# Two double-bank PSUM tiles taken in turn by a pair's first products, and a gate row that is turned on TensorE before it is written

## The chip, the cores and the metric

The kernel runs on one core of one Trainium2 chip. The metric is device time in microseconds (us) of one execution. Three runs of the kernel before gave 1339.73, 1339.51 and 1337.06 us, with a median of 1339.51. The profiled execution is another one, and took 1336.35 us.

## The reference, cut to what matters

One decoder block over 1024 tokens of width 1024. A vector `c` modulates the normed input, one wide projection feeds two mixers, and their gated sum goes through a last matrix:

```python
mod = jax.nn.silu(c) @ ada_w[l] + ada_b[l]
shift, scale, gate = jnp.split(mod, 3, axis=-1)
h = rms_norm(x, norm_w[l]) * (1.0 + scale[:, None]) + shift[:, None]
proj = h @ w_in[l]
...
merged = jax.nn.sigmoid(ga) * y_a + jax.nn.sigmoid(gb) * y_b
x = x + gate[:, None] * (merged @ w_out[l])
return rms_norm(x, final_norm_w)
```

Mixer A is a gated delta rule (a recurrence over chunks, 8 heads), mixer B a windowed attention. The change touches two places: how the columns of `proj` that hold the gates z and g are multiplied, and how `gate` gets from a column layout in SBUF to a row in DRAM.

## The kernel before, in words

Every large product is done in three passes of fp32r matmuls (high part by high, high by low, low by high), 512 columns each. The order of all instructions is worked out when the kernel is built: each part of the work is a generator ("stream") with a priority, and a planner (`Sched`, with a table of assumed durations) steps whichever stream of the highest priority it holds to be ready. What a stream issues in a step gets its place in the queue of its engine at once. On the chip each engine then keeps that order, and waits with semaphores where data or a buffer is not ready. The program records each instruction through one helper, so the profile puts all of them on line 106; they are told apart by their tiles.

Buffers are slots: `big` (34 tiles of 128x1024), `mid` (6 of 128x512), `sq` (6 of 128x128), `wr` and `wh` for raw and split weights. PSUM has two double-bank tiles `pj` (128x1024, 4 KiB in a partition) and four single-bank tiles `sb` (128x512).

**The pairs.** 14 pairs of weight tiles (z and most of g) are multiplied by a scheme of seven products in place of eight (`PRODUCTS`, line 32): each product is 4 k-tiles of 3 matmuls, 12 matmuls of 128x512. `pair` (line 661) issues them in order. Products 1 and 2 (into `ps["B11"]` and `ps["T2"]`) go to the two halves of one `pj` tile, products 3 and 4 (`T1`, `B21`) to the two halves of the other, and products 5 to 7 to `sb` tiles. A stream of higher priority, `pair_out` (line 695), follows and turns the products into four output blocks: as soon as a product is issued, its evacuation is issued. That is a copy on ScalarE (ACT) for the first product and an addition on VectorE (DVE) for each of the others, `mid<-mid,pj` in the profile. A `pj` tile is given back with `pj.put()` when the second of its two products has been read. Before the first pair, the operand T1 is prepared in `t1_part` (line 805); after the last pair, `h_blocks` (line 739) restores the blocks that the pairs had overwritten, and the first unit after the pairs waits for them.

**The modulation.** `ada_stream` (line 475) computes `mod` with one VectorE dot product per 128 rows of `ada_w`. After the normed input is ready, it does the last eight (the gate), halves them (line 492) and writes them with one DMA (line 493) from `mod[:, 16:24]`, 128 partitions with 8 elements each, to the row `row_d` in DRAM: the address pattern puts elements of one partition 512 B apart, so each of the 1024 elements of 4 B is a run of its own. The row is read once, near the end (`rows_stream`).

**What stands near it in the queues.** Right behind that DMA, SyncE's queue (SP) issues two loads `big<-grow` (`d_stream`, line 1165): 512 KB each, the decay logits of a head broadcast to 128 partitions. VectorE scans them (`tensor_tensor_scan`), and behind the scans in its queue come the key scales and the convolution of a key tile (`conv`, line 838: three `scalar_tensor_tensor` that read a `pj` tile, then `pj.put()`). The stream `stats_stream` (line 1099) does with a 128x64 tile what the change does with the gate: transpose on TensorE, ACT copy, DMA in rows (`grow<-sq`).

Of the kernel before, what the change touches and what calls it, by code (L numbers as in the profile page):

```python
# [9 lines left out]
AF = mybir.ActivationFunctionType  # L10
OP = mybir.AluOpType
# [4 lines left out]
P = 128  # L16
# [12 lines left out]
HALVES = (slice(0, 512), slice(512, 1024))  # L29
# [235 lines left out]
def hybrid_block_kernel(ctx: ExitStack, tc: tile.TileContext, x, c, norm_w, ada_w, ada_b, w_tiles, w_vb0, w_vb1,  # L265
# [3 lines left out]
    pe, act, dve, pool, sp = S.pe, S.act, S.dve, S.pool, S.sp  # L269
# [16 lines left out]
    sq = Slots(S, smp, "sq", 6, [P, P])  # L286
    pj = Slots(S, pjp, "pj", 2, [P, T])
    sb = Slots(S, sbp, "sb", 4, [P, 512])

    def const(shape, name, dtype=F32):  # L290
        return cp.tile(shape, dtype, name=name)
# [3 lines left out]
    ident, upper, later, ones = cst[:, 0:128], cst[:, 128:256], cst[:, 256:384], cst[:, 384:512]  # L295
# [10 lines left out]
    mod = const([P, 24], "mod")  # L306
# [28 lines left out]
    row_d = dp.tile([1, T], F32, name="rowd")  # L335
# [133 lines left out]
    def ada_dot(j, aw):  # L469
        mdt = yield from big.get()  # L470
        dve.scalar_tensor_tensor(mdt, aw, 1.0, scb[0], op0=OP.mult, op1=OP.mult, accum_out=mod[:, j:j + 1])
        dve.tensor_tensor(mod[:, j:j + 1], mod[:, j:j + 1], adab[:, j:j + 1], op=OP.add)
        big.put()

    def ada_stream():
        for kk in range(8):
            yield ev_mod
            for j in (8 + kk, kk):
                yield ev_aw[j]
                yield from ada_dot(j, aw[j])  # L480
                big.put()
            dve.scalar_tensor_tensor(A_d[:, kk:kk + 1], mod[:, 8 + kk:9 + kk], 1.0, nw_t[:, kk:kk + 1],
                                     op0=OP.add, op1=OP.mult)
            S.set(ada_ev[kk])
        yield ev_h[7][1]
        for j in range(16, 24):
            a_ = yield from big.get()
            sp.dma_start(a_, ada_w[j * P:(j + 1) * P, :])
            yield
            yield from ada_dot(j, a_)  # L490
            big.put()
        dve.tensor_scalar(mod[:, 16:24], mod[:, 16:24], 0.5, None, op0=OP.mult)
        sp.dma_start(row_d.rearrange("o (j p) -> p (o j)", p=P), mod[:, 16:24])
        big.put()

    todo_h = []
    for k_ in range(8 + LAG):
# [163 lines left out]
    def pair(u, blocks, ready, sink, free=None):  # L661

        nk = u.n // 2 // P
        ps = {}
        done = {b: Event() for _, b in PRODUCTS}
        S.add(pair_out(ps, done, sink), 8, "pairout")
        for n, (a, b) in enumerate(PRODUCTS):
            if n in (0, 2):  # L670
                two = yield from pj.get()
            if n > 3:
                pt = yield from sb.get()
            else:
                pt = two[:, HALVES[n % 2]]
            ps[b] = pt
            yield u.ev[a]
            w, v = u.part[a]
            for kt in range(nk):
                yield ready[b][kt]  # L680
                whi, wlo = w[:, kt * P:(kt + 1) * P], v[:, kt * P:(kt + 1) * P]
                hi, lo = blocks[b][kt]
                pe.matmul(pt, whi, hi, start=kt == 0, stop=False)
                pe.matmul(pt, whi, lo, start=False, stop=False)
                pe.matmul(pt, wlo, hi, start=False, stop=kt == nk - 1)
                if free:
                    free(b, kt)
                yield S.now()
            if a in ("S1", "A12", "A22"):
                wh.put(2)  # L690
            elif a == "S4":
                wh.put()
            S.set(done[b])

    def pair_out(ps, done, sink):
        def add(o, x, y):
            dve.tensor_tensor(o, x, y, op=OP.add)

        yield done["B11"]
        p, u, v = yield from mid.many(3)  # L700
        act.activation(p, ps["B11"], AF.Copy)
        yield done["T2"]
        add(u, p, ps["T2"])
        pj.put()
        yield done["T1"]
        add(v, u, ps["T1"])
        yield done["B21"]
        add(p, p, ps["B21"])
        pj.put()
        yield  # L710
        yield from sink(0, 0, p)
        yield done["T3"]
        add(p, v, ps["T3"])
        add(u, u, ps["T3"])
        sb.put()
        yield
        yield from sink(1, 1, p)
        mid.put()
        yield done["B22"]
        add(v, v, ps["B22"])  # L720
        sb.put()
        yield
        yield from sink(0, 1, v)
        mid.put()
        yield done["T4"]
        add(u, u, ps["T4"])
        sb.put()
        yield
        yield from sink(1, 0, u)
        mid.put()  # L730
# [267 lines left out]
    def projections():  # L998
# [41 lines left out]
        for n, (kind, idx, u) in enumerate(prog):  # L1040
# [3 lines left out]
            if kind == "two":  # L1044
                if n == LAST2:
                    yield from pair(u, HB, ev_hb, idx, h_free)
                    big.debt -= 1
                    S.set(ev_early)
                else:
                    yield from pair(u, HB, ev_hb, idx)  # L1050
                continue
# [944 lines left out]
    S.add(load_start(), 0, "load")  # L1996
    S.add(ln_start(), 0, "ln")
    S.add(ada_stream(), 1, "ada")
    S.add(h_stream(), 1, "ha")
    S.add(h_stream(), 1.1, "hb")  # L2000
# [94 lines left out]
```

## Time and profile before

| what | value |
|---|---|
| median of three runs | 1339.51 us |
| profiled execution | 1336.35 us, its span 1334.6 us |
| TensorE (PE) busy | 1252.5 us, 94% of the span |
| VectorE busy | 749.5 us, 56% |
| ScalarE busy | 532.1 us, 40% |
| GpSimd (POOL) busy | 382.6 us, 29% |
| 128x512 matmuls into pj | x3168, mean 404 ns of one |

A mean of 404 ns does not mean that a matmul begins every 404 ns: matmuls are pipelined, and in a stream a new one begins before the last has ended. In the timeline a row is a run of instructions of one kind on one engine: start, length, operation, shapes, count, and in brackets the idle time of the engine just before it and what ended that idle time. Engine names with a q are queues.

### The profile page before, as it was taken

The numbers are of one execution on the slowest core, as the hardware profiler recorded it, in microseconds if no ns is written. First come the engines' busy times: TensorE is split into PE (matmuls) and PEld (weight loads), VectorE is DVE, ScalarE is ACT, GpSimd is POOL, SyncE is SP. The second block draws the span as 40 slices with busy tenths as digits, with TensorE's granted clock in tenths as the row PEclk, the third lists the DMA queues.
The fourth block names the chain that finished last, engine by engine and source line by source line (L and its number), as shares of the span: only waits on it lengthen the run. The fifth ranks groups of instructions, "written<-read, shape, count | busy, mean of one in ns | idle before, by whom it ended". The sixth has DMA issues, their size and how long they took to land. (4 is left out here: it accounts for less than half of the span.)

```text
span 1334.6 us, 19368 instructions
## 1 busy us (share of the span) xinstructions
PE 1252.5 (94%) x7218; PEld 1028.3 (77%) x7218; DVE 749.5 (56%) x1412; ACT 532.1 (40%) x1140; POOL 382.6 (29%) x227
## 2 busy tenths in 40 slices
PE   5798899989999899999989999999999999999997
PEld 3597788857887677777768888888988767888886
DVE  6655688975556464644546787244442336756533
ACT  5545453333443343544436532355363452212211
POOL 4621854652122121311234511212124102222400
PEclk9899899989999999999989999999999999999999
DMA  9354547644444745542435634656856758653422
GB/s 362 131 177 125 177 132 218 215 141 145 150 130 159 218 135 162 187 155 71 135 127 159 196 103 150 214 166 215 244 178 200 243 182 227 198 185 123 142 95 95
DMA packets 141328, 225.79 MB, mean 169 GB/s; under 512 B 34193, under 2 KB 83761, under 8 KB 141234
## 3 DMA queue, kind: packets, MB, share of 16 engines
q1 hardware_dynamic: 141090, 224.29, 52.7%
q8 instruction: 57, 0.93, 0.3%
q14 instruction: 37, 0.30, 0.1%
q10 hardware_dynamic: 144, 0.26, 0.1%
HBM read 149.88 MB, written 74.63 MB: 168 GB/s over the span
## 5 line engine op out<-in xcount | busy, mean ns | idle before, releaser
L106 PE MATMUL pj<-big,wh 128*128 128x512 f32 x3168 | 806.8, 404 | 48.1 <-DVE mid L106 12.5
L106 PEld LDWEIGHTS pj<-big,wh 128*128 128x128 f32 x3168 | 587.6, 192 | 182.2 <-DVE mid L106 18.0
L106 POOL TENSOR_TENSOR wh<-wr,wh 128x1024 fp32r<-128x1024 f32 (+4 forms) x64 | 145.4, 2273 | 446.9 <-ACT wh L106 389.3
L106 ACT ACTIVATE wh<-wr 128x1024 fp32r<-128x1024 f32 (+4 forms) x110 | 104.2, 948 | 157.7 <-PE pj L106 112.5
L106 PE MATMUL sb<-big,wh 128*128 128x512 f32 x504 | 130.0, 402 | 0.2 <-DVE mid L106 0.2
L106 ACT ACTIVATE big<-big 128x1024 f32<-128x1024 f32 (+1 forms) x61 | 64.6, 1059 | 158.8 <-DVE big L106 126.9
L106 PE MATMUL pj<-wh,big 128*128 128x256 f32 (+2 forms) x702 | 107.2, 309 | 3.5 <-DVE big L106 1.8
L106 PEld LDWEIGHTS sb<-big,wh 128*128 128x128 f32 x504 | 91.3, 189 | 19.3 <-DVE mid L106 1.2
L106 PEld LDWEIGHTS pj<-wh,big 128*128 128x128 f32 x702 | 96.4, 193 | 10.8 <-issue 3.1
L106 DVE SCALAR_TENSOR_TENSOR big<-pj,cw,big 128x1023 f32<-128x1023 f32 (+2 forms) x66 | 84.5, 1280 | 29.9 <-ACT big L106 28.2
L106 POOL TENSOR_TENSOR big<-wr 128x512 f32<-128x512 f32 x14 | 20.6, 1471 | 243.0 <-DMA wr<-in_w_tiles_dram 166.0
L106 DVE TENSOR_TENSOR big<-big,big 128x1024 f32<-128x1024 f32 (+3 forms) x40 | 62.5, 1568 | 24.3 <-ACT big L106 13.0
L106 PEld LDWEIGHTS sb<-sq,big 128*128 128x128 f32 x464 | 65.0, 190 | 12.1 <-issue 3.2
L106 PE MATMUL sb<-sq,big 128*128 128x128 f32 x464 | 69.2, 278 | 2.5 <-DVE sq L106 2.0
L106 ACT ACTIVATE mid<-sb 128x384 f32<-128x384 f32 (+5 forms) x75 | 34.4, 461 | 81.3 <-PE sb L106 66.1
L106 DVE TENSOR_TENSOR mid<-mid,pj 128x512 f32<-128x512 f32 x42 | 28.8, 687 | 61.7 <-PE pj L106 57.3
L106 POOL TENSOR_TENSOR big<-mid,big 128x512 fp32r<-128x512 f32 x32 | 50.5, 1584 | 37.5 <-ACT big L106 22.3
L106 DVE TENSOR_TENSOR wh<-wr,wh 128x1024 fp32r<-128x1024 f32 (+1 forms) x46 | 51.9, 1131 | 7.4 <-ACT wh L106 7.2
L106 DVE TENSOR_TENSOR mid<-mid,sb 128x512 f32<-128x512 f32 x56 | 37.0, 682 | 33.3 <-DMA zd<-mid 14.3
L106 ACT ACTIVATE mid<-mid 128x512 f32<-128x512 f32 (+1 forms) x59 | 35.9, 609 | 47.7 <-DVE mid L106 47.3
L106 ACT ACTIVATE mid<-mid,sta 128x128 f32<-128x128 f32 (+1 forms) x96 | 42.1, 440 | 27.0 <-DVE sta L106 26.9
L106 DVE SCALAR_TENSOR_TENSOR sq<-sb,gsm,big 128x128 f32<-128x128 f32 x56 | 19.4, 348 | 53.3 <-PE sb L106 49.4
(138 smaller groups left out, 1451.2 us busy)
## 6 DMA issues: line engine op xcount, KB each, us to landing
wr<-in_w_tiles_dram SPq DMA_DIRECT2D x64, 512.0 KB, 4.1
rkd<-big SPq DMA_DIRECT2D x32, 512.0 KB, 4.5
big<-rkd SPq DMA_DIRECT2D x64, 256.0 KB, 3.5
big<-in_ada_w_dram SPq DMA_DIRECT2D x24, 512.0 KB, 9.0
big<-in_x_dram SPq DMA_DIRECT2D x16, 512.0 KB, 4.6
big<-gd SPq DMA_DIRECT2D x16, 512.0 KB, 4.9
zd<-mid SPq DMA_DIRECT2D x28, 256.0 KB, 3.3
big<-zd SPq DMA_DIRECT2D x14, 512.0 KB, 7.5
```

The costliest lines, as they stand in the source:

```text
L106: r = f(*a, **k)
```

## The change

The first four products of a pair take the two `pj` tiles in turn: product 1 the lower half of the first tile, product 2 the lower half of the second, products 3 and 4 the upper halves. Both tiles are taken before the second product, and the first tile is given back after the third product's addition, where it was after the second's.

The gate is no longer halved on VectorE. Its 128x8 tile is transposed on TensorE into an `sb` tile, copied with a factor of 0.5 by ScalarE into an `sq` tile of 8 rows, and written from there, 8 rows of 512 B. The `big` tile that held the broadcast `c` is given back before these steps.

```diff
-        dve.tensor_scalar(mod[:, 16:24], mod[:, 16:24], 0.5, None, op0=OP.mult)
-        sp.dma_start(row_d.rearrange("o (j p) -> p (o j)", p=P), mod[:, 16:24])
         big.put()
+        yield
+        pb = yield from sb.get()
+        pe.transpose(pb[0:8, 0:P], mod[:, 16:24], ident)
+        yield
+        t = yield from sq.get()
+        act.activation(t[0:8, :], pb[0:8, 0:P], AF.Copy, scale=0.5)
+        sb.put()
+        yield
+        sp.dma_start(row_d.rearrange("o (j p) -> (o j) p", p=P), t[0:8, :])
+        sq.put()
...
-        ps = {}
+        ps, two = {}, []
...
         for n, (a, b) in enumerate(PRODUCTS):
-            if n in (0, 2):
-                two = yield from pj.get()
+            if n < 2:
+                two.append((yield from pj.get()))
             if n > 3:
                 pt = yield from sb.get()
             else:
-                pt = two[:, HALVES[n % 2]]
+                pt = two[n % 2][:, HALVES[n // 2]]
...
         add(u, p, ps["T2"])
-        pj.put()
         yield done["T1"]
         add(v, u, ps["T1"])
+        pj.put()
         yield done["B21"]
         add(p, p, ps["B21"])
         pj.put()
```

## Prediction

> **What bounds the kernel now.** I read the page first, then the waits of TensorE, then the timeline around the two places that the change touches.
>
> ```profile
> span 1334.6 us, 19368 instructions
> PE 1252.5 (94%) x7218; PEld 1028.3 (77%) x7218; DVE 749.5 (56%) x1412; ACT 532.1 (40%) x1140; POOL 382.6 (29%) x227
> L106 PE MATMUL pj<-big,wh 128*128 128x512 f32 x3168 | 806.8, 404 | 48.1 <-DVE mid L106 12.5
> ```
> ```profile
> PE pj L106 <- DVE big L106: 13.5, 6, 8.6
> PE pj L106 <- DVE mid L106: 12.5, 14, 2.4
> PE pj L106 <- ACT mid L106: 8.6, 11, 1.4
> ...
> PE pj L106 <- ACT big L106: 5.9, 3, 2.9
> ...
> PE sb L106 <- DVE sq L106: 4.7, 2, 2.7
> ```
>
> TensorE is the bound: no other engine is busy over 56%, and TensorE has only some 82 us in which it does nothing. So an idle microsecond of TensorE that goes away is worth nearly a microsecond of the end, as long as nothing else comes late in its place. The second list (total us, times, longest) tells where that idle time is. Two rows stand out by their counts: 14 waits for `DVE mid` and 11 for `ACT mid`, where the kernel has 14 pairs. And one wait is far longer than the rest: 8.6 us for `DVE big`. The change aims at exactly these.
>
> **The pairs.** One pair in the timeline:
>
> ```profile
> 400.55 2.32 PE L106 MATMUL pj<-big,wh 128*128 128x512 f32 x9
> 402.91 0.60 ACT L106 ACTIVATE mid<-pj 128x512 f32<-128x512 f32 x1 [1.01 <-PE pj L106]
> 403.56 5.05 PE L106 MATMUL pj<-big,wh 128*128 128x512 f32 x21 [0.69 <-ACT mid L106]
> 406.68 0.69 DVE L106 TENSOR_TENSOR mid<-mid,pj 128x512 f32<-128x512 f32 x1 [0.24 <-PE pj L106]
> 410.57 0.69 DVE L106 TENSOR_TENSOR mid<-mid,pj 128x512 f32<-128x512 f32 x1 [3.20 <-PE pj L106]
> 411.31 1.65 PE L106 MATMUL pj<-big,wh 128*128 128x512 f32 x6 [0.78 <-DVE mid L106]
> ```
>
> Product 1 ends; ACT copies it from 402.91 to 403.51, and only at 403.56 does product 2 begin. It goes to the other half of the same PSUM tile, so the program holds the write back until the read of the tile is over. Then 21 matmuls run without a break: 12 of product 2 and 9 of product 3. Product 2 is read by DVE at 406.68, in the midst of this run, and nothing waits: product 3 writes the other tile. Product 4 goes to the tile from which product 3 is being read (410.57), and waits again. So a write waits for a read of the same tile, whichever half, and not for one of the other tile. With the tiles taken in turn, product 2 no longer shares a tile with product 1, nor product 4 with product 3. The new neighbours are products 1 and 3, and 2 and 4, and between their turns lies a whole product.
>
> What one wait costs is more than its bracket:
>
> ```profile
> 280.71 3.01 PE L106 MATMUL pj<-big,wh 128*128 128x512 f32 x12 [0.75 <-ACT mid L106]
> 286.25 0.80 PE L106 MATMUL pj<-big,wh 128*128 128x512 f32 x1 [2.53 <-ACT big L106]
> ...
> 295.65 4.61 PE L106 MATMUL pj<-big,wh 128*128 128x512 f32 x12 [2.37 <-DVE mid L106]
> 300.10 8.36 PE L106 MATMUL sb<-big,wh 128*128 128x512 f32 x36
> 308.30 2.88 PE L106 MATMUL pj<-big,wh 128*128 128x512 f32 x12
> ...
> 677.58 0.73 PE L106 MATMUL pj<-big,wh 128*128 128x512 f32 x2 [2.94 <-ACT big L106]
> ```
>
> 36 matmuls without a break take 8.36 us, so one begins every 0.227 us ((8.36 - 0.40) / 35), while one lasts 0.404. The bracket is counted from the end of the last one, and leaves out 0.404 - 0.227 = 0.18 us that a stream would have overlapped. And 12 matmuls right after a wait take 3.01 us, others 2.88: 0.13 more. A wait thus costs its bracket and 0.31. All 25: 12.5 + 8.6 + 25 x 0.31 = 28.9 us.
>
> Two of them I take as not gained, 1.1 us each (0.75 or 0.78 and 0.31). In the first pair (280.71 to 295.65) product 3 waits 2.53 us for its operand T1, which ACT is still splitting (`ACT big`); a product 2 that begins earlier only lengthens that wait. After the last pair the next unit waits for restored blocks (677.58, 2.94 us), and a pair that ends earlier will wait the longer. So 26.7 us go.
>
> What is late next: product 3 now needs the copy of product 1, issued one product earlier, and product 4 needs the addition of product 2. A product is 12 x 0.227 = 2.7 us; the read takes 0.7, and the copy above began 0.04 us after the last matmul's end (402.87). So the reader may be some 1.7 us late (2.7 - 0.18 - 0.04 - 0.7, less the step between engines) before TensorE waits. The row at 295.65 shows that it can be: product 4 of the first pair waited 2.37 us, because DVE was in a long chain. And each recurrence step between the pairs loses the slack that a pair's waits gave it. I give back 3 us for all of this, near the 4.7 us in 2 waits that `DVE sq` costs now; the ends are 0 and 10 (about a third of what was won). **Pairs: 23.7 us.**
>
> [...]
>
> **The gate's row.**
>
> ```profile
> 113.28 0.16 DVE L106 TENSOR_TENSOR mod<-mod,adab 128x1 f32<-128x1 f32 x1
> 113.48 0.17 DVE L106 TENSOR_SCALAR mod<-mod 128x8 f32<-128x8 f32 x1
> 113.68 0.38 SPq L106 DMA_DIRECT2D rowd<-mod  x1
> 114.16 1.78 SPq L106 DMA_DIRECT2D big<-grow  x2
> ...
> 120.03 17.84 SPq L106 DMA_DIRECT2D rkd<-big  x2
> ...
> 122.83 6.64 PE L106 MATMUL pj<-big,wh 128*128 128x512 f32 x28
> 128.28 5.16 DVE L106 TENSOR_TENSOR_SCAN big<-big,cst 128x128 f32<-128x128 f32 x16 [14.63 <-DMA big<-grow]
> ...
> 134.05 3.91 DVE L106 SCALAR_TENSOR_TENSOR big<-pj,cw,big 128x1023 f32<-128x1023 f32 x3
> ```
> ```profile
> 138.10 9.14 PE L106 MATMUL pj<-big,wh 128*128 128x512 f32 x30 [8.63 <-DVE big L106]
> ```
> ```profile
> 114.00:123.00 9.00, 9.00 (x50) 7.62 (x49) 0.00 (x0) 8.69 (x29) 0.00 (x0) 1.00 0.18 12
> 123.00:129.50 6.50, 6.47 (x29) 4.99 (x27) 1.23 (x4) 3.92 (x11) 0.00 (x0) 1.00 0.86 215
> ...
> 138.00:142.00 4.00, 3.90 (x9) 3.14 (x10) 3.86 (x6) 3.04 (x11) 3.65 (x3) 0.50 0.72 183
> ...
> 280.00:680.00 400.00, 364.84 (x2173) 289.45 (x2173) 218.40 (x410) 160.96 (x361) 92.36 (x59) 0.98 0.49 153
> ```
> ```profile
> big<-grow SPq DMA_DIRECT2D x8, 512.0 KB, 6.5
> ...
> grow<-sq SPq DMA_DIRECT2D x1, 32.0 KB, 1.8
> ...
> rowd<-mod SPq DMA_DIRECT2D x1, 4.0 KB, 9.3
> ```
>
> The chain: the row's DMA is issued at 113.68 and lands 9.3 us later, at 123.0. The two loads behind it are issued at 114.16, but until 123 the DMA engines move 12 GB/s at 18% busy; from then on 215. The loads move only when the row is through, though the row is 4 KB. DVE stands idle for 14.63 us, scans from 128.28, reaches the convolution at 134.05 and frees the `pj` tile at 137.96; TensorE, out of work at 129.47, goes on at 138.10. And it goes on slowly: in the four microseconds after (column before the last two: granted clock 0.50) nine matmuls take what they would do in 9 x 0.227 = 2.0 us. The wait costs 8.63 + 0.31 + 2.0 = 10.9 us.
>
> After the change the row is 8 runs of 512 B. The nearest row is `grow<-sq`, the same kind of write from the same kind of tile, 64 rows, 32 KB: 1.8 us. The loads would land in the 6.5 us that is the median of all eight. If they are issued at 114.16 again, the scan begins near 120.7. From scan to the end of the convolution it is 137.96 - 128.28 = 9.7 us, so the tile is free near 130.4, where TensorE needs it at 129.5: 0.9 us of wait are left. With nothing else on the DMA engines the load can be faster, down to no wait; I take 0.5. An idle time this short does not slow what follows: the 2.53 us above lie in a stretch whose granted clock is 0.98.
>
> What is added:
>
> ```profile
> 101.26 0.30 PE L106 MATMUL sb<-cst,gsm 128*64 128x128 f32 x1 [0.61 <-DVE gsm L106]
> 101.80 0.25 ACT L106 ACTIVATE sq<-sb 64x128 f32<-64x128 f32 x1
> ```
>
> The model is the decay row in `stats_stream`: 0.30 us on TensorE with 0.61 us of wait, 0.25 us on ACT. The transpose stands in TensorE's order and everything of TensorE stands behind it, so if its place comes before DVE has finished `mod` (113.44) TensorE waits. Bounds: 0.1 us (pipelined, no wait) to 0.9. The four `sb` tiles are then in use by the key transposes, whose evacuations the planner must see first, so its place is a little later than 113.44; I take 0.4 with the ACT copy, which other ACT work covers. On SP the row's DMA now waits for ACT; behind it stand the writes `rkd<-big`, the second of which waits long anyway (17.84 us for the two). If the loads `grow` stay behind it, they are late by about the time of transpose, copy and their queues, some 3 us, and the price is 3 us of TensorE's wait. DVE loses 0.17 us, worth nothing. The row is read near the end of the span, so its landing does not matter. **Gate: 10.9 - 0.5 - 0.4 = 10.0 us.**
>
> **Sum.** 23.7 + 10.0 = 33.7 us. From the profiled execution, 1336.35 - 33.7 = 1302.7. That execution is 3.2 us below the median of the runs, so by the median 1339.5 - 33.7 = 1305.8: 1306.
>
> **Rivals.**
>
> The gate's half fails: the loads are slow for themselves, or the transpose costs as a new wait what the row's DMA cost. For it: the median landing of `big<-grow`, 6.5, is already not short. Against it: 12 GB/s until the moment the row lands. Time: 1339.5 - 23.7 = 1316. Chance 0.08.
>
> The pairs' half does nothing, because the wait hangs on something other than the tile. [...] Against it: product 3 runs through a read of the other tile. Time: 1339.5 - 10.0 = 1329.5. Chance 0.05.
>
> Slower, through the recurrence:
>
> ```profile
> L106 PE MATMUL sb<-sq,TT x112: 270/274/377, 343.6 to 1017.6; 128*128 128x128 f32 x112
> ```
>
> All orders are planned anew behind the change, and recurrence steps lie between the products. 112 such matmuls are 56 steps of two instructions each after the first of every head; each step has three links over DVE or ACT, 168 links. If TensorE, without the pairs' pauses, comes to every link over 0.2 us too early, 168 x 0.2 = 33.6 us, and the gain is gone; at 0.25 us the kernel takes 1339.5 + 8 = 1348. Against it: only 4.7 us in 2 such waits now. Chance 0.04. Half of that lateness, 0.1 us a link, gives 1306 + 17 = 1323, chance 0.03.
>
> [...] The clock of 0.98 from 280 to 680, with 25 pauses that the change removes, speaks against it: chance 0.01.
>
> **How the numbers follow.** My forecast has 0.77. Its own range is 1299 (nothing given back, no wait left: 28.9 - 2.2 + 10.9 = 37.6, and 3 us for runs as low as the profiled one) to 1313 (10 us given back). The range must reach the first rival, and ends at 1319. A measurement of this kernel can tell about 0.2% (2.7 us) from no change. Every case but two is faster by more; the slower one and the clock have 0.05, and no change has 0.02, the recurrence at its point of balance. So faster 0.93.
>
> **What would show it.** In the profile after: no `ACT mid` waits of `PE pj` or only one or two, and `DVE mid` under 4 us; `rowd<-sq` in the list of DMAs, landing in 2 to 3 us; the scan from about 120 us; no idle time of TensorE above 1 us between 100 and 200 us, and a granted clock near 1.0 there. Wrong would be: waits of the same count with other partners (products 3 and 4), the scan still at 128, more `DVE sq` waits than two, or a gap before a transpose `sb<-cst,mod`.

## The result, and the profile after

The kernel after takes 1304.46 us (median of 4 runs, 1303.67 to 1305.68). Beside it the kernel before has 1338.28 us (4 runs, 1335.88 to 1339.73). The ratio is 0.975, with a 95% interval from 0.9731 to 0.9768. The forecast was 1306, in a range of 1299 to 1319. The profiled execution after took 1305.68 us, 30.7 us less than the one before.

The page of the kernel after, its span, its engines and the group of the 128x512 matmuls:

```profile
span 1304.0 us, 19379 instructions
PE 1241.0 (95%) x7219; PEld 1027.7 (79%) x7219; DVE 756.8 (58%) x1411; ACT 532.0 (41%) x1141; POOL 380.4 (29%) x227
L106 PE MATMUL pj<-big,wh 128*128 128x512 f32 x3168 | 794.7, 401 | 27.1 <-ACT big L106 13.8
```

TensorE's idle time, span less busy, went from 82 to 63 us. Its busy time fell too, by 11.5 us, though it does one instruction more. A busy microsecond is not a fixed amount of work: in the kernel after a 128x512 matmul lasted 652 ns at a granted clock of 0.50 (649.94 to 653) and 389 ns at 1.00 (284 to 288), and the end of the last matmul ahead of a wait, of which a stream overlaps some 0.18 us (one of 0.404 us begins every 0.227), counts as busy. The waits of TensorE, kernel after (total us, times, longest):

```profile
PE pj L106 <- ACT big L106: 14.3, 4, 7.9
...
PE sb L106 <- DVE sq L106: 7.2, 2, 3.9
...
PE pj L106 <- DVE big L106: 4.2, 5, 2.1
...
PE pj L106 <- ACT mid L106: 0.7, 1, 0.7
```

Of the 14 waits for `DVE mid` before a `pj` product none is left, of the 11 for `ACT mid` one, and the 8.6 us for `DVE big` are gone. Two things have grown. `ACT big` has a wait of 7.9 us that was not there, and `DVE sq` has 7.2 where it had 4.7.

Around the modulation, the timeline of the kernel after:

```profile
108.01 0.80 SPq L106 DMA_DIRECT2D big<-grow  x2
113.73 5.16 DVE L106 TENSOR_TENSOR_SCAN big<-big,cst 128x128 f32<-128x128 f32 x16 [1.30 <-DMA big<-grow]
...
116.06 0.27 PE L106 MATMUL sb<-cst,mod 128*8 128x128 f32 x1
...
121.11 0.29 SPq L106 DMA_DIRECT2D rowd<-sq  x1
...
123.07 3.92 DVE L106 SCALAR_TENSOR_TENSOR big<-pj,cw,big 128x1023 f32<-128x1023 f32 x3 [1.76 <-ACT big L106]
```

The loads are now issued at 108.01, six microseconds earlier than before. SP's queue had stood at the row, which waited for `mod`; the row's place is now behind them. The scan begins at 113.73 (before: 128.28) and the convolution at 123.07 (134.05). The transpose waits for nothing. The windows of the kernel after (PE, PEld, DVE, ACT, POOL busy, granted clock, DMA share, GB/s):

```profile
129.50:138.00 8.50, 8.50 (x50) 7.40 (x49) 6.18 (x5) 6.87 (x14) 8.50 (x5) 1.00 0.25 80
138.00:142.00 4.00, 4.00 (x30) 3.60 (x29) 3.96 (x10) 1.00 (x6) 3.42 (x2) 1.00 0.55 152
280.00:680.00 400.00, 385.36 (x2303) 315.30 (x2302) 219.65 (x423) 171.62 (x383) 91.58 (x57) 0.98 0.49 155
```

From 129.5 to 138, where TensorE had stood, it is busy throughout, and from 138 to 142 it does 30 matmuls at a granted clock of 1.00 (most of them of 128x128) instead of nine at 0.50.

The first pair has a wait of a new kind. Timeline of the kernel after:

```profile
267.94 1.22 DVE L106 TENSOR_TENSOR big<-big,ik 128x1024 f32<-128x1024 f32 x1
...
269.19 0.32 SPq L106 DMA_DIRECT2D vrd<-big  x1
269.56 2.56 SPq L106 DMA_DIRECT2D mid<-t1d  x4
...
275.58 1.29 ACT L106 ACTIVATE big<-mid 128x512 fp32r<-128x512 f32 x2 [0.89 <-DMA mid<-t1d]
...
277.72 1.00 ACT L106 ACTIVATE big<-pj 128x1024 f32<-128x1024 f32 x1
...
278.78 10.09 PE L106 MATMUL pj<-big,wh 128*128 128x512 f32 x36 [7.88 <-ACT big L106]
288.70 3.56 PE L106 MATMUL sb<-big,wh 128*128 128x512 f32 x15
```

Read it from the bottom. Product 2 now needs the second `pj` tile, which still holds the result of the unit before. ACT copies that result out at 277.72. But in ACT's queue the copy stands behind the splits of T1, and these wait for the loads `mid<-t1d`. On SP those loads were issued only at 269.56, behind a store `vrd<-big` that waited for DVE. So TensorE stands for 7.88 us. Before, the same pair had four waits (0.75, 2.53, 0.63 and 2.37 us). Now it has one, and in this trace the pair as a whole is still 2.3 us shorter. That is not firm: in a second profile of the same kernel, from the run again below, the loads are issued at 271.69, the wait is 9.85 us, and the pair is 0.1 us longer than before.

**Where the time went**, by the starts and ends of the same instructions in both traces. Product 5 of the first pair starts at 300.10 before and at 288.70 after, 11.4 us earlier. Of these, 1.0 us had been won by the transpose of the decay row (101.26 and 100.25), 8.1 came from there to the first pair, 2.3 in it. From product 5 of the first pair to the end of product 7 of the last it takes 369.3 and 350.2 us, 19.1 less. From there to the end of the span 665.2 and 665.1. Sum: 30.6 us of span. Each of these is a difference of two single executions.

### The profile page after: what moved, and what is told of

The parts are those of the page before. It is cut to its first block, busy times and chain, and to the rows that moved or that the text cites. A ratio compares the mean times of both kernels' runs of the same rounds, so it can differ in the third digit from the quotient of the medians.

```text
span 1304.0 us, 19379 instructions
## 1 busy us (share of the span) xinstructions
PE 1241.0 (95%) x7219; PEld 1027.7 (79%) x7219; DVE 756.8 (58%) x1411; ACT 532.0 (41%) x1141; POOL 380.4 (29%) x227
## 4 chain that ended last, share of the span: by engine, by line
PE 43%; DVE 4%; DMA 2%; issue 1%; ACT 0%; SPq 0%; POOL 0%; POOLq 0%; DVEq 0%; ACTq 0%
PE pj L106 35%; PE sb L106 8%; DVE big L106 3%; DVE mid L106 1%; DMA mid<-fgd 1%; DMA big<-rkd 1%; DMA ogd<-mid 0%; ACT big L106 0%; DVE qpart L106 0%; SPq L106 0%; DVE fga L106 0%; POOL big L106 0%; ACT mid L106 0%; POOLq L2099 0%; ACT wh L106 0%
## 5 line engine op out<-in xcount | busy, mean ns | idle before, releaser
L106 PE MATMUL pj<-big,wh 128*128 128x512 f32 x3168 | 794.7, 401 | 27.1 <-ACT big L106 13.8
L106 PE MATMUL pj<-big,big 128*128 128x512 f32 x210 | 49.1, 389 | 0.0
```

What stands on the lines that cost most here:

```text
L106: r = f(*a, **k)
```

## The experiments

In each, "after" is the kernel after and "before" the kernel before; ratios are to the kernel before, timed beside it.

### The pairs' half alone

The kernel before, with the change's edits in `pair` and `pair_out` and none in `ada_stream`:

```diff
-            if n in (0, 2):
-                two = yield from pj.get()
+            if n < 2:
+                two.append((yield from pj.get()))
...
-                pt = two[:, HALVES[n % 2]]
+                pt = two[n % 2][:, HALVES[n // 2]]
```

> The kernel before with the pairs' half of the change alone; the gate's row stays as it was. Theory (a write to a PSUM tile waits for a read of the same tile, whichever half): the 14 waits for DVE mid and 11 for ACT mid of PE pj go, the 8.6 us wait for DVE big at 138 us stays, and about 21 us are won: 1338.3 - 21 = 1317. Rival (the gain of the change comes from the new order that the planner makes, not from the tiles): much less than 15 us is won here, because the order is much as before up to the pairs.

1321.18 us, ratio 0.9857 (0.9835 to 0.9878): 18.4 us less. The waits for `ACT mid` and `DVE mid` before a `pj` product are gone, and the one behind the row stays (timeline of this kernel):

```profile
138.58 3.64 PE L106 MATMUL pj<-big,wh 128*128 128x512 f32 x9 [9.52 <-DVE big L106]
```

So this half does what it says by itself. It gains less than the 23.7 of the forecast, in part for reasons taken up below, and in part because this kernel has a wait of its own, 3.77 us for `ACT wh` at 310.23.

### The gate's half alone

The kernel before, with the change's edits in `ada_stream` alone:

```diff
-        sp.dma_start(row_d.rearrange("o (j p) -> p (o j)", p=P), mod[:, 16:24])
...
+        pe.transpose(pb[0:8, 0:P], mod[:, 16:24], ident)
...
+        act.activation(t[0:8, :], pb[0:8, 0:P], AF.Copy, scale=0.5)
...
+        sp.dma_start(row_d.rearrange("o (j p) -> (o j) p", p=P), t[0:8, :])
```

> The kernel before with the gate's half alone. Theory (the two loads of decay logits stood behind the row's 1024 runs of 4 B): the wait of 8.6 us at 138 us goes and the clock stays up there, about 10 us are won: 1338.3 - 10 = 1328. The 25 waits in the pairs stay. Rival (the halves hang together: time won before the pairs is lost again at the first pair, where the operand T1 is late): 1334 or more, with a longer wait at the first pair.

1331.98 us, ratio 0.9934 (0.9913 to 0.9954): 7.6 us less. No wait is left at 138. But the first pair has a longer one (timeline of this kernel):

```profile
281.76 6.12 PE L106 MATMUL pj<-big,wh 128*128 128x512 f32 x15 [6.41 <-ACT mid L106]
```

TensorE comes to the first pair earlier and there waits 6.41 us where it had waited 0.75, for the copy of product 1, which stands in ACT's queue behind the splits of T1. A part of this half's gain is given back there. The halves add up to 26.0 us, and together they bring 33.8; the product of their ratios, 0.979, lies just above the interval of the whole. The 6.41 us here and the 3.77 us of the pairs' half are waits that the kernel after does not have.

### Another neighbour in the tile

The kernel after, where products 2 and 3 share a tile instead of 1 and 3, 2 and 4:

```diff
-                pt = two[n % 2][:, HALVES[n // 2]]
+                pt = two[n in (1, 2)][:, HALVES[n // 2]]
```

> The changed kernel, but product 3 goes to the upper half of the second tile and product 4 to that of the first: product 2 and product 3 are neighbours in one tile, all four still lie in four banks, and products 1 and 2 and 3 and 4 are still in different tiles. Theory (guard by tile): product 3 waits for the addition that reads product 2, about 13 or 14 waits for DVE mid of 0.8 us, 0.18 to 0.31 us more each: 13 to 15 us slower than the changed kernel, 1304.5 + 14 = 1318. Rival (the guard goes by bank, and the waits of before came from something else about products 2 and 4): no such waits, 1304.5.

1322.38 us, ratio 0.9866 (0.9845 to 0.9887). By the ratios (0.975 for the kernel after) some 15.5 us are lost. The waits of TensorE in this kernel:

```profile
PE pj L106 <- DVE mid L106: 11.3, 13, 1.3
```

All that differs in the code is which half of which tile a product takes. Thirteen waits come with it, 11.3 us in all, one in nearly every pair, at product 3, whose neighbour is being read. The program holds back a write to a tile while any part of it is read. Products 2 and 3 lie in different halves of the tile. Whether the chip would do without these waits was not tried; the program's guard is per tile, and that is what costs here.

### The copy of the unit before ahead of T1

The kernel after, where the splits of T1 are issued only when the copy that frees the second tile has been:

```diff
+    ev_evac = Event()
-        yield ev_last[i]
+        yield [ev_last[i], ev_evac]
...
+        if store is KB and i == 1:
+            S.set(ev_evac)
```

> The changed kernel, with the ScalarE splits of T1 held back, in the order of issue, until the copy is issued that frees the second PSUM tile before the first pair. Theory (the new wait of 7.9 us at the first pair is the second tile, asked for one product earlier than before, and its copy stands in ScalarE's queue behind splits that wait for late loads): product 2 of the first pair begins within 1.5 us of product 1's end, product 3 then waits some microseconds for T1, and the first pair ends 3 to 6 us earlier: 1304.5 - 4.5 = 1300. Rival (what is late is T1 itself, and the wait only moves from product 2 to product 3): 1304.5 within 1.

1313.44 us, ratio 0.9796 (0.9776 to 0.9815): about 6 us slower than the kernel after, where I had expected it faster. Timeline of this kernel:

```profile
276.27 5.32 PE L106 MATMUL pj<-big,wh 128*128 128x512 f32 x15 [3.93 <-ACT big L106]
282.33 2.34 PE L106 MATMUL pj<-big,wh 128*128 128x512 f32 x9 [0.75 <-ACT mid L106]
287.74 5.49 PE L106 MATMUL pj<-big,wh 128*128 128x512 f32 x12 [3.07 <-DVE mid L106]
```

One wait of 7.88 us has become three of 3.93, 0.75 and 3.07 us. ACT's timeline in the same kernel tells why the first is still there:

```profile
273.73 0.63 ACT L106 ACTIVATE big<-mid 128x512 fp32r<-128x512 f32 x1 [6.90 <-DVE mid L106]
...
275.21 1.00 ACT L106 ACTIVATE big<-pj 128x1024 f32<-128x1024 f32 x1
```

The copy now stands ahead of the splits that wait for loads, but ACT stands before it all the same, in another step whose data comes from DVE. And at product 4 DVE is late. My theory, that the order of the copy and the splits is all that holds the pair, fell. As I read it, without a further run that shows it, the pair stands in the midst of a stretch in which ACT, DVE and SP all work in a fixed order, and a step pulled ahead on one of them meets the next.

### The row where it was, but later in the queue

The kernel before, with the old row (1024 runs of 4 B, no transpose), issued only after the decay of the second head has been issued:

```diff
-        sp.dma_start(row_d.rearrange("o (j p) -> p (o j)", p=P), mod[:, 16:24])
         big.put()
+        yield ev_d[1]
+        sp.dma_start(row_d.rearrange("o (j p) -> p (o j)", p=P), mod[:, 16:24])
```

> The kernel before; the gate is halved on VectorE and written with 1024 runs of 4 B as before, but the DMA is issued only after the decay loads and their scans have been issued. Theory (only what stands behind the row's DMA in the queue is late): the loads are issued some 6 us earlier than before, because SyncE's queue no longer waits for the gate, and land in 6 us; the wait of 8.6 us at 138 us is gone and the time is that of the gate's half alone, 1332. Rival (the 1024 short runs cost wherever they stand): another stall of several us shows further down, and the time is 1336 or more.

1328.08 us, ratio 0.9919 (0.9891 to 0.9947): as good as the gate's half with its transpose. The row is issued at 131.87, the loads at 108.46, and TensorE has no wait over 0.25 us between 105 and 260. The loads land 6.2 us after their issue, and the next two writes `rkd<-big` (from 119.49 on, still ahead of the row) 3.5 us after theirs (median). In the kernel before, behind the row, it is 14.0 us for the loads and 11.0 for the write `rkd<-big` issued at 120.03. The place in the queue is enough.

### The turned row ahead of the loads

The gate's half, with the loads held until the turned row has been issued:

```diff
+        S.set(ev_rowd)
...
-        yield [ev_g, ev_stats]
+        yield [ev_g, ev_stats, ev_rowd]
```

> The gate's half alone, but the decay loads are held back until the gate's row has been issued (turned, 8 runs of 512 B). Theory (the place of the row in the queue is worth as much as its runs): the loads are issued after the copy on ScalarE, near 121 us, land near 127, and TensorE waits 7 to 9 us as before: 1338 to 1341. Rival (the runs were the whole cost): the loads land within 7 us of the gate's dot product, near 120 us, and the time stays at 1332.

1328.15 us, ratio 0.9916 (0.9891 to 0.994). I had expected 1338 or more, and was wrong. The loads are late, yet TensorE hardly waits there (timeline of this kernel):

```profile
121.70 0.81 SPq L106 DMA_DIRECT2D big<-grow  x2
123.30 3.92 DVE L106 SCALAR_TENSOR_TENSOR big<-pj,cw,big 128x1023 f32<-128x1023 f32 x3 [1.76 <-ACT big L106]
...
127.86 8.96 DVE L106 TENSOR_TENSOR_SCAN big<-big,cst 128x128 f32<-128x128 f32 x16
...
141.50 2.06 PE L106 MATMUL pj<-big,wh 128*128 128x512 f32 x8 [0.85 <-DVE big L106]
```

The scans run from 127.86, as late as in the kernel before. But the convolution that frees the `pj` tile now stands ahead of them on DVE: with the loads issued so late, the plan has it first. In the kernel before the plan had the scans first, and the convolution, which needs nothing of them, stood behind an instruction that waited 14.63 us for its load. So the 8.6 us are not the price of a late scan. They are the price of a scan that is late in a queue whose order was planned without that lateness.

### The row twice, and an eighth of it

The kernel before, with the old row written twice ahead of the loads:

```diff
+    row2_d = dp.tile([1, T], F32, name="rowe")
...
-        sp.dma_start(row_d.rearrange("o (j p) -> p (o j)", p=P), mod[:, 16:24])
+        for r in (row2_d, row_d):
+            sp.dma_start(r.rearrange("o (j p) -> p (o j)", p=P), mod[:, 16:24])
```

> The kernel before, with the row of 1024 runs of 4 B written twice in front of the decay loads (the second time to a row that nothing reads). Theory (the loads wait until the runs are through, about 9 us a row): the scan begins 8 to 10 us later, near 137 us, the wait of TensorE grows from 8.6 to 16 to 19 us, and the time is 1339.6 + 9 = 1348. Rival (the loads were late only because SyncE's queue stood until the gate was computed): the second row adds its issue alone, 0.5 us: 1340.

The kernel before, with 128 runs of 4 B (to a scratch row) ahead of the loads, and the whole row late:

```diff
+    row2_d = dp.tile([1, T], F32, name="rowe")
...
-        sp.dma_start(row_d.rearrange("o (j p) -> p (o j)", p=P), mod[:, 16:24])
         big.put()
+        sp.dma_start(row2_d.rearrange("o (j p) -> p (o j)", p=P)[:, 0:1], mod[:, 16:17])
+        yield ev_d[1]
+        sp.dma_start(row_d.rearrange("o (j p) -> p (o j)", p=P), mod[:, 16:24])
```

> The kernel before, with one eighth of the row (128 runs of 4 B, to a row that nothing reads) in front of the decay loads, and the whole row written later, where it did no harm. Theory (a write of short runs holds up what follows for a time that hardly depends on how many there are, since two rows held it up no longer than one): the loads land 12 to 14 us after their issue, TensorE waits 7 to 9 us, 1338. Rival (the hold-up grows with the runs, but two rows are worked on side by side): the loads land within 8 us of their issue, TensorE waits under 3 us, 1330.

Twice: 1338.73 us, ratio 1.0 (0.9978 to 1.0022). An eighth: 1337.29 us, ratio 0.9997 (0.9977 to 1.0017). Neither moves the time, where I had expected 1348 of the row twice, and a price in proportion to the runs is excluded. (The profiled execution with the row twice took 1348.55, ten above its median; only its DMA rows are used.) The DMA issues from 108 to 131, median us from issue to landing, first of the kernel before, then with the row twice, with an eighth, and of the kernel after:

```profile
big<-grow SPq DMA_DIRECT2D x2, 512.0 KB, 14.0
...
rowd<-mod SPq DMA_DIRECT2D x1, 4.0 KB, 9.3
```
```profile
big<-grow SPq DMA_DIRECT2D x2, 512.0 KB, 14.7
...
rowe<-mod SPq DMA_DIRECT2D x1, 4.0 KB, 10.0
rowd<-mod SPq DMA_DIRECT2D x1, 4.0 KB, 11.6
```
```profile
big<-grow SPq DMA_DIRECT2D x2, 512.0 KB, 12.7
...
rowe<-mod SPq DMA_DIRECT2D x1, 0.5 KB, 7.7
```
```profile
big<-grow SPq DMA_DIRECT2D x2, 512.0 KB, 6.1
```

Loads behind 128, 1024 or 2048 runs of 4 B land 12.7, 14.0 and 14.7 us after their issue; with none ahead 6.1, and 4.3 behind the eight runs of 512 B of the kernel with the turned row ahead. In these traces there is a hold-up of 6.6 to 8.6 us (12.7 and 14.7 less 6.1) that comes with such a write and differs little with its length. That it comes from the row, and not from something else at that time, the kernel with the row late shows: there, with no such write ahead of them, the loads land after 6.2 us and the writes from 119.49 on after 3.5. What makes it stays open: no view here shows what the DMA engines wait for in it.

### The first pair's wait, a second attempt

The kernel after, where the second half of one value stream, whose store `vrd<-big` holds SP, is issued behind T1's loads:

```diff
+        if h == 3:
+            yield ev_hb["T1"]
```

> The changed kernel, with the second half of the fourth value stream held back until T1 is prepared, so that its write does not stand in front of T1's loads in SyncE's queue. Theory (the 7.9 us of the first pair come from T1's loads, which stand behind that write, which waits for VectorE): the loads are issued 3 to 6 us earlier, the wait falls to 2 to 5 us, the granted clock does not fall, and the time is 1304.5 - 4 = 1300. Rival (VectorE's inversion chain and the PSUM tile hold the first pair anyway): within 2 us of the changed kernel.

1303.32 us, ratio 0.9731 (0.9706 to 0.9756). Timeline of this kernel:

```profile
274.64 7.05 PE L106 MATMUL pj<-big,wh 128*128 128x512 f32 x24 [3.38 <-ACT big L106]
283.14 3.04 PE L106 MATMUL pj<-big,wh 128*128 128x512 f32 x12 [1.45 <-DVE mid L106]
```

3.38 and 1.45 us of wait in place of 7.88, with T1's loads issued at 262.26 in place of 269.56: the store on SP was indeed what held them. But the granted clock fell behind this wait too (0.50 in the two microseconds after it), where I had expected that it would not. The span is 3.1 us shorter than that of the kernel after, but the intervals overlap, and the time lies within the 2 us that I had named for the rival; from the time alone the two kernels can't be told apart.

### Cover for the restored blocks, alone and together

After the last pair the next unit needs the restored blocks in its k-tiles 0 to 3. Here it takes k-tiles 4 to 7 first, once alone, and once with the edit before; beside the second the kernel after was run again.

```diff
-            for kk in range(8):
+            for q in range(8):
+                kk = (q + 4) % 8 if n == LAST2 + 1 else q
...
-                yield from three(..., *hT[kk], kk == 0, kk == 7)
+                yield from three(..., *hT[kk], q == 0, q == 7)
```

> The changed kernel again, beside the next one on one chip, so that the two can be compared: 0.975 of the kernel before, 1305 us.

> The changed kernel with the fourth value stream held back as before, and with the first unit after the pairs beginning with the four k-tiles that are not restored. Theory (the 5.5 us wait after the last pair stands for restored blocks, and six matmuls a k-tile, 5.4 us, cover it): that wait goes to under 1 us, and the first pair's stays at 3.4: 4 to 7 us faster than the changed kernel, near 1299. Rival (the restored blocks come later still, since they follow the pair's end): the wait only moves to the fifth k-tile, 1303.

> The kernel after, where only the first unit after the pairs takes its k-tiles 4 to 7 first (they need no restored blocks); the value load of the first pair is left where it was. Theory, each edit acts at its own place: after the last product of the pairs the span loses what it lost with both edits (from 665.1 to about 658 us, that is 7 to 8 us), the wait of 4.27 us for ACT big and that of 1.25 us for DVE big become one of about 1 us, and the first pair's wait of 8 to 10 us stays: 1297 to 1299 us, ratio to the kernel before 0.969 to 0.972. Rival, the two edits only pay together (the gain of 9 us came from the orders being planned anew): over 1301 us, or a stretch of pairs that is shorter or longer by over 3 us.

The kernel after again: 1305.4 us, ratio 0.975 (0.9724 to 0.9776). Both edits: 1296.17 us, ratio 0.9682 (0.9661 to 0.9704), faster than both kernels, by 9.2 us than the kernel after beside it. The cover alone: 1301.86 us, ratio 0.9706 (0.9678 to 0.9735), between the two, with an interval that touches both. Timelines behind the last pair, of the kernel after and of the cover alone:

```profile
647.48 1.21 PE L106 MATMUL pj<-big,wh 128*128 128x512 f32 x2 [4.27 <-ACT big L106]
649.94 6.44 PE L106 MATMUL pj<-big,wh 128*128 128x512 f32 x18 [1.25 <-DVE big L106]
```
```profile
638.37 10.36 PE L106 MATMUL pj<-big,wh 128*128 128x512 f32 x45
649.65 6.66 PE L106 MATMUL pj<-big,wh 128*128 128x512 f32 x28 [0.92 <-DVE big L106]
```

From the end of the last product 7 to the end of the span it takes 665.1 us in the kernel after, 658.9 with the cover alone and 658.0 with both. The first pair's wait stays at 9.19 us with the cover alone. So by the traces each edit acts at its own place, as the theory had it. The times leave it open: the median of the cover alone, 1301.86, meets the sign that I had named for the rival (over 1301), while its ratio, 0.9706, lies in the range named for the theory (0.969 to 0.972), and its profiled execution took 1299.10. The waits that go are 4.6 us (4.27 + 1.25 - 0.92). By the start of the transposes that come next (667.34 and 659.55) 7.4 us are won, and 1.2 of them are lost again further on. What was won beyond the waits is mostly clock. The window from 640 to 660 in the kernel after, and with the cover alone:

```profile
640.00:660.00 20.00, 14.48 (x52) 10.93 (x51) 6.78 (x10) 4.38 (x6) 6.49 (x4) 0.83 0.39 128
```
```profile
640.00:660.00 20.00, 19.08 (x87) 15.48 (x86) 13.26 (x21) 7.80 (x10) 7.77 (x4) 1.00 0.49 152
```

A mean of 0.83 over 20 us is 3.4 us of clock lost, a part of it in time in which TensorE stood still and lost nothing by it.

## Why the prediction was right, and where it wasn't

**What bounds the kernel:** right. TensorE's waits went and the end moved with them.

**The pairs: right in mechanism, 2.2 us too large.** The guard is by tile, as the experiment with another neighbour shows. Predicted were 23.7 us; measured in the traces 2.3 in the first pair, 19.1 in the others and 0.1 behind the last, 21.5 in all. The second profile of the kernel after, held against the same one of the kernel before, has -0.1, 20.6 and -0.7, 19.8 in all. By its parts:
- The first pair, 2.7 predicted (the wait of 2.37 at product 4). The sum is near in the one trace, by luck (in the other it is -0.1), and the way is not: I had product 2 begin earlier and product 3 wait for T1. But product 2 now needs the second tile, which before was needed one product later. The change says so (both tiles are taken before the second product), and I did not follow it to who frees that tile.
- The other pairs: brackets of 18.0 us in 23 waits went (12.5 + 8.6, less 0.75 and 2.37 of the first pair). At 0.31 more for each it would have been 25.2, less 3 given back 22.2. It was 19.1. Waits that grew or came (`DVE sq` 7.2 for 4.7, one of 0.7 for `ACT mid`, one of 0.3) took back 3.5, so that 3 was well sized; what a wait cost beyond its bracket comes out at (19.1 - 18.0 + 3.5) / 23 = 0.20, not 0.31. That figure has in it the clock that the grown waits cost, below.
- Behind the last pair I let 1.1 us be swallowed. Nothing was: the chain of the restored blocks starts from the pair's own products and moves with them; its waits are 5.52 us after and 5.28 before.

**The gate: right to 2 us, by a partly wrong route.** The wait of 8.63 us went, with the half clock behind it. Three steps came out otherwise. The loads were not issued at 114.16 again but at 108.01, since SP no longer stands at the row; with that no rest of a wait was left (predicted 0.5). The transpose cost no wait (predicted 0.4). And a wait of 1.68 us at 173.24 and one of 0.27 at 235.25 came up instead, on the way to the first pair, which the kernel with the gate's half alone shows too: 10.9 less 1.68 and 0.27, and less 0.31 for each of the two as the prediction reckons a wait, is 8.3, near the 8.1 that were measured. That the row itself holds the loads is right, but for the wait two things had to come together, and I had seen only the first: the short runs (the turned row ahead of the loads does not hold them), and an order on DVE that reckoned with early loads.

**"An idle time this short does not slow what follows": wrong.** I argued it from a clock of 0.98 over 400 us, in which a few microseconds at half clock can't be seen. Windows of 2 us, laid behind each wait, show them. The kernel before, behind the waits of 2.53, 2.37 (its second 2 us), 2.72 and 2.00 us:

```profile
286.20:288.00 1.80, 1.12 (x2) 0.61 (x3) 1.77 (x3) 0.63 (x1) 1.72 (x2) 0.50 0.49 141
...
297.60:299.60 2.00, 2.00 (x6) 1.59 (x5) 0.00 (x0) 0.00 (x0) 0.00 (x0) 0.51 0.99 293
```
```profile
457.80:459.80 2.00, 1.91 (x10) 1.66 (x11) 1.23 (x3) 1.94 (x5) 1.20 (x1) 1.00 0.16 61
...
514.20:516.20 2.00, 2.00 (x8) 1.71 (x9) 2.00 (x5) 0.40 (x2) 0.00 (x0) 0.60 0.36 135
```

The kernel after, behind 1.68 us, 3.32, 4.27 with 1.25, and 7.88:

```profile
173.20:175.00 1.80, 1.76 (x8) 1.49 (x9) 1.77 (x6) 1.78 (x3) 1.80 (x2) 1.00 0.97 292
...
435.70:437.70 2.00, 1.93 (x6) 1.64 (x7) 1.22 (x3) 1.95 (x5) 1.22 (x1) 0.55 0.10 41
...
649.90:651.90 2.00, 1.96 (x5) 1.58 (x6) 0.00 (x0) 0.00 (x0) 0.00 (x0) 0.50 0.00 0
...
278.70:280.70 2.00, 1.92 (x5) 1.54 (x6) 1.90 (x5) 0.51 (x2) 0.60 (x1) 0.50 0.56 233
```

The column before the last two is the granted clock. Behind waits of 2.00, 2.37 and 2.53 us it is 0.5 to 0.6, as it is behind 4.27 and 7.88; behind 2.72 us at 457.8 it stayed at 1.00. The length alone does not decide it. In the kernel before, the clock is 0.67 in the two microseconds behind a wait of 1.84 us (at 814.30), and 0.50 behind one of 1.20 us (at 323.85) that follows two microseconds of 32x32 matmuls. And one and the same wait, 2.07 us for `DVE big`, has half clock behind it in the kernel after and none in the second profile of that kernel:

```profile
783.80:785.80 2.00, 2.00 (x10) 2.00 (x11) 1.93 (x4) 1.01 (x1) 0.00 (x0) 0.56 0.08 31
```
```profile
784.14:786.14 2.00, 2.00 (x17) 2.00 (x18) 1.93 (x4) 1.01 (x1) 0.00 (x0) 1.00 0.08 31
```

Ten matmuls in two microseconds stand against seventeen. What decides it, no run here shows. In the trace of the kernel before, the first pair paid twice for half clock, and in that of the kernel after only once, which is how one wait of 7.88 us can be cheaper than four that sum to 6.28. The error did not move the gate's term, as no rest of a wait was left there. It left out a cost that I estimate at 1.5 to 2 us (2 us times what the granted clock lacks to 1, summed over the two windows behind a wait: 0.64 and 0.51 behind 2.37 us, 0.50 and 0.50 behind 3.89 us at 491.50 in the kernel after, 0.50 and 0.74 behind the 1.20 us at 323.85) at most waits of 2 us or more elsewhere, and at some shorter ones: at 435.77 a wait that grew from 2.72 to 3.32 us now has a clock of 0.55 behind it, where it was 1.00.

**The sum.** Of the span 30.6 us went, of the medians 33.8 (1338.28 to 1304.46). The forecast of 33.7 meets the second and is 3 us too large for the first, on which it was worked out (pairs 2.2, gate 1.9, against 1.0 won at the start that no edit explains). The profiled execution before lay 1.9 us below its median and the one after 1.2 above, which is the difference. The closeness of 1306 to 1304.46 is in part luck; the terms were right to 2 to 4 us each.

**The signs.** Of those that I had named, the waits, the clock and the scan came as said or better. The idle time of 1.68 us at 173.24 is one that should not have been, and of `rowd<-sq` the trace has no landing.

**The rivals.** None came true. A failing gate half and a failing pairs half are excluded by each half's own run. More waits in the recurrence there are, 2.5 us in place of the 17 to 42 of that rival. That the clock would be half throughout the pairs, at a chance of 0.01, no run shows: its mean from 280 to 680 was 0.98 in both kernels.

## What to carry to other kernels

Where a program guards a tile as a whole, lay products that follow each other in different tiles, and then look at what the second tile was doing one product earlier. When a wait on one engine is traced to a late DMA, ask first why the waiting work stands behind it in a fixed order: here, moving the DMA cured it, and so did the other order. Look for lost clock in windows of 2 us behind each wait, not in a mean over a stage.

## What the runs showed of the hardware

- Writes of 4 B runs held up the two loads of 512 KB behind them in the same queue by 6.6 to 8.6 us, with little difference between 128, 1024 and 2048 runs (12.7, 14.0 and 14.7 us to landing, 6.1 in the kernel after, without), where eight runs of 512 B did not (4.3). Each figure is from one trace.
- TensorE's granted clock was 0.67 in the first and 0.50 in the second two microseconds behind an idle time of 1.84 us (at 814.30 in the kernel before), and it did not fall behind each longer one: it stayed at 1.00 behind 2.72 us (at 457.89 in the same kernel), and the same wait of 2.07 us had 0.56 behind it in one execution of the kernel after and 1.00 in another. What decides it is not shown.
